# A hybrid convolution and attention block: values through DRAM, gates stored as logits, a product on GpSimd, and two PSUM banks in place of three for attention

## The chip, the cores and the metric

The kernel runs on one NeuronCore of a Trainium2 chip. The metric is the device time of one execution in microseconds (us). Five engines work side by side, each through its own queue in order: TensorE (PE, with its weight loads shown as PEld), VectorE (DVE), ScalarE (ACT), GpSimd (POOL) and SyncE (SP), which issues the DMAs. TensorE writes into PSUM, eight banks of 512 float32 columns on 128 partitions each; every other tile lies in SBUF.

## The reference, cut to what matters

One layer over 2048 rows of 1024 channels, in float32. A projection of 7680 columns feeds two branches that are merged:

```python
h = rmsnorm(x, norm_g)
glu_in, conv_gate, q, k, v, attn_gate, merge_logits = split(h @ w_in)
c = silu(layernorm(depthwise_conv_31_taps(a * sigmoid(b))))       # a, b = halves of glu_in
y_conv = (c * silu(conv_gate)) @ w_conv_out
a = sliding_window_attention(rope(q), rope(k), v, sinks)          # 16 heads of 64, 4 key/value heads
y_attn = (a * silu(attn_gate)) @ w_attn_out                       # window 128, a sink per head
g_conv, g_attn = split(sigmoid(merge_logits))
x = x + (g_conv * y_conv + g_attn * y_attn) @ w_out
out = rmsnorm(x, final_norm_g)
```

Attention takes blocks of 128 queries against the keys of their own block and of the one before. A softmax over the window has the sink of the head in its denominator.

## The kernel before

Each float32 operand of a product is split into a rounded part and a remainder (`hi` and `lo`, both float32r), and each product is three matmuls: hi by hi, hi by lo, lo by hi. The rows are taken in two sweeps `s` of 1024 (`T`), each in two halves of 512. Channels lie on partitions, rows along the free dimension.

A sweep runs through `program()`: rotary projections of k and q and the v projection, then 32 projections of gates (`ag` for attention, `cg` for the convolution, `ma` and `mc` for the merge), with the eight channel tiles of the gated unit (`gb`, `ga`) put in between, then `ya` (attention's output product), `yc` (the convolution's) and `o` (the last). A projection of 128 columns and 512 rows is 24 matmuls into one PSUM tile of the pool `mm_ps`. Gates are activated as they leave PSUM and go to DRAM (`spill`); `load_gate` brings them back during `ya`, `yc` and in `u_op`.

The order on TensorE is the order in which the program is written. A planner, `Line`, cuts into the projections: after every three matmuls `spend` looks for work that is due, which is a step of a chain (attention, layer norm, transposes) or an operation in the background (31 vector operations for each channel tile of the convolution, whose running sum `acc` lies in two PSUM banks of `cv_ps`). The order on the other engines comes from a scheduler.

Attention is 32 units per sweep, `attention(n)`, for each key/value head `g` and query block `b`; one begins every 13.8 us by the planner's count. A unit has three steps on TensorE:

1. scores: two PSUM tiles `sc` of two heads each, four matmuls into each, one tile straight after the other. ScalarE copies one half of each into SBUF (L581), VectorE copies the other half under the causal mask (L582). Maximum, exponentials and division follow in SBUF (`ss`, `st`).
2. 22 us later four transposes into the PSUM tile `tpp`, read by ScalarE and VectorE as the hi and lo parts `pt` (L607, L242). `pc` is `pt` under a mask, made on GpSimd.
3. 16 us later the product with the values into the PSUM tile `ov`: `pt` times the values of the block before, `pc` times the difference of the two blocks' values (`vt`, `vd`). It leaves PSUM in four steps that follow one another: a copy of one half on ScalarE (L625), an addition of the other on VectorE (L626), and the same for the second pair of heads. Then the gate's product (L627), a split into hi and lo, and a store to `d_a`.

By the time that step 3 of unit n-3 is due, step 1 of unit n is due too. So `ov` of one unit and the two `sc` tiles of another stand close together on TensorE, with three projection matmuls between them or none. All of `sc`, `tpp`, `ov` and the transposes of the input and the values take their PSUM tiles from the pool `tp_ps`, which has three banks, and `mm_ps` has three.

`tile_pool(bufs=n)` gives out n buffers for one tag: a tile is written when some earlier tile's readers are done with the buffer that it gets.

Of the kernel before, what the change touches and what calls it, by code (L numbers as in the profile page):

```python
# [12 lines left out]
F32 = mybir.dt.float32  # L13
F32R = mybir.dt.float32r
I32 = mybir.dt.int32
AF = mybir.ActivationFunctionType
ALU = mybir.AluOpType
AX = mybir.AxisListType

P = 128  # L20
S = 2048
D = 1024
KC = D // P
T = 1024
NSWEEP = S // T
NB = T // P
TH = 512
TAPS = 31
HALO = TAPS - 1
HD = 64  # L30
NH = 16
NKV = 4
# [21 lines left out]
def hybrid_block(ctx: ExitStack, tc: tile.TileContext, x, par_d, w_in, w_conv, sinks, w_attn, w_out,  # L54
                 fin_g, rope_t, out):
    nc = tc.nc
# [3 lines left out]
    slots = ctx.enter_context(tc.tile_pool(name="slots", bufs=1))  # L60
    stage = ctx.enter_context(tc.tile_pool(name="stage", bufs=4))
    work = ctx.enter_context(tc.tile_pool(name="work", bufs=2))
    mm_ps = ctx.enter_context(tc.tile_pool(name="mm_ps", bufs=3, space=bass.MemoryType.PSUM))
    tp_ps = ctx.enter_context(tc.tile_pool(name="tp_ps", bufs=3, space=bass.MemoryType.PSUM))
    cv_ps = ctx.enter_context(tc.tile_pool(name="cv_ps", bufs=1, space=bass.MemoryType.PSUM))
    dram = ctx.enter_context(tc.tile_pool(name="dram", bufs=1, space=bass.MemoryType.DRAM))

# [3 lines left out]
    def f(ap):  # L71
        return ap.bitcast(F32)
# [2 lines left out]
    H = [f"h{i}" for i in range(16)]  # L75
    A = [f"a{i}" for i in range(16)]
    C = [f"c{i}" for i in range(8)]
    X = [f"x{i}" for i in range(3)]
    WIDE = set(C) | {"a14", "a15", "h14", "h15"}

    def slot(tag, shape, dt, name):
        n = int(np.prod(shape[1:]))
        full = HALO + T + 2 if tag in WIDE else 1024
        t = slots.tile([P, full], dt, tag=tag, name=name)
        v = t[:, 0:n]
        if len(shape) == 3:
            v = v.rearrange("p (a b) -> p a b", b=shape[2])
        elif len(shape) == 4:
            v = v.rearrange("p (a b c) -> p a b c", b=shape[2], c=shape[3])
        return v  # L90
# [6 lines left out]
    def next_of(key, tags):  # L97
        rot.setdefault(key, cycle(range(len(tags))))
        return tags[next(rot[key])]
# [59 lines left out]
    d_k = dram.tile([2, 2, P, S], F32, name="d_k")  # L159

    d_a = dram.tile([NSWEEP * KC, P, 2, T], F32, name="d_a")
    v_halo = const.tile([P, NKV, 2, HD], F32R, name="v_halo")
    v_last = const.tile([P, 2, P], F32, name="v_last")
    dve.memset(v_last, 0.0)

# [1 line left out]
    class Line:  # L167
        t = 0.0
# [72 lines left out]
    def split_lo(out_, full, hi, eng):  # L241
        eng.tensor_tensor(out=out_, in0=full, in1=f(hi), op=ALU.subtract)  # L242
# [129 lines left out]
    def sweep(s):  # L372
# [61 lines left out]
        def gate_item(kind, col, func, e):  # L434
            def ev(half, ps):
                g = t2k(f"{kind}{s}_{e}_{half}")
                act.activation(out=g, in_=ps, func=func)
                nc.sync.dma_start(out=spill[kind][s * KC + e, :, half * TH:(half + 1) * TH], in_=g)
                if half == 1:
                    stored.add((kind, e))  # L440

            return project(w_in[col // P + e], h_rhs, f"{kind}{s}_{e}", ev)

        def load_gate(kind, e, half):
            g = t2k(f"l{kind}{s}_{e}_{half}")
            nc.sync.dma_start(out=g, in_=spill[kind][s * KC + e, :, half * TH:(half + 1) * TH])
            return g


# [42 lines left out]
            return store  # L492


        vt, vd = {}, {}

        def v_item(i):
            def chain(half, vs):
                yield 0.0, 7.0
                tp = tp_ps.tile([P, 4, P], F32, tag="tp", name=f"tpv{s}_{i}_{half}")  # L500
                for j in range(4):
                    pe.transpose(out=tp[:, j, :], in_=vs[:, j * P:(j + 1) * P], identity=ident)
                vf, d = (t2k(f"{n}{s}_{i}_{half}").rearrange("p (b c) -> p b c", c=P) for n in ("vf", "vd"))
                act.copy(vf, tp)
                dve.tensor_tensor(out=d[:, 1:4], in0=tp[:, 1:4], in1=vf[:, 0:3], op=ALU.subtract)
                dve.tensor_tensor(out=d[:, 0], in0=tp[:, 0], in1=v_last[:, i], op=ALU.subtract)
                act.copy(v_last[:, i], vf[:, 3])
                for j in range(2):
                    bp = 2 * half + j
                    if i == 0:  # L510
                        vt[bp] = slot(AT[bp], [P, 2, NKV, 2 * HD], F32R, f"vt{s}_{bp}")
                        vd[bp] = slot((X + AT[15:])[bp], [P, 2, NKV, 2 * HD], F32R, f"vd{s}_{bp}")
                    for full, to in ((tp, vt), (d, vd)):
                        part = full[:, 2 * j:2 * j + 2, :].rearrange("p b (g d) -> p b g d", d=HD)
                        hi, lo = (to[bp][:, :, 2 * i:2 * i + 2, a * HD:(a + 1) * HD] for a in range(2))
                        act.copy(hi, part)
                        split_lo(lo, part, hi, dve)
                yield 0.44, 0.0

            def ev(half, ps):  # L520
                vs = t2k(f"vs{s}_{i}_{half}")
                act.copy(vs, ps)
                line.start(chain(half, vs))

            return project(w_in[C_V // P + i], h_rhs, f"v{i}{s}", ev)

        def v_of(g, b):
            if b < 0:
                return v_halo[:, g]
            return vt[b // 2][:, b % 2, g, :]  # L530


        done, qk = {}, {}
# [20 lines left out]
        def attention(n):  # L554
# [52 lines left out]
            act.copy(pt[:, 0], tpp)  # L607
            split_lo(pt[:, 1], tpp, pt[:, 0], dve)
            if first:
                seq = [(v_of(g, b), pt)]  # L610
            else:
                pc = slot(next_of("pc", AT[9:11]), [P, 2, GQ, P], F32R, f"pc{u}")
                pool.affine_select(out=pc, in_=f(pt), pattern=[[0, 2], [0, GQ], [1, P]],  # L613
                                   compare_op=ALU.is_ge, fill=0.0, base=0, channel_multiplier=-1)
                seq = [(v_of(g, b - 1), pt), (vd[b // 2][:, b % 2, g, :], pc)]
            yield 0.44, LAT[1]

            ov = tp_ps.tile([P, GQ, P], F32, tag="tp", name=f"ov{u}")
            nm = 2 * len(seq)
            for i in range(nm):  # L620
                vv, pp = seq[i // 2]
                pe.matmul(out=ov, lhsT=vv, rhs=pp[:, i % 2], start=(i == 0), stop=(i == nm - 1))  # L622
            ovp = ov.rearrange("p (i r) q -> p i r q", r=2)
            for r, own, other in ((0, slice(0, HD), slice(HD, P)), (1, slice(HD, P), slice(0, HD))):
                act.copy(oT[own], ovp[other, :, r, :])  # L625
                dve.tensor_tensor(out=oT[own], in0=ovp[own, :, r, :], in1=oT[own], op=ALU.add)  # L626
            dve.tensor_tensor(out=oT, in0=oT, in1=ga, op=ALU.mult)  # L627
            hl = sb.rearrange("p (l c) q -> p l c q", c=2)
            act.copy(hl[:, 0].bitcast(F32R), oT)
            split_lo(hl[:, 1].bitcast(F32R), oT, hl[:, 0], dve)  # L630
            for i in range(2):
                nc.sync.dma_start(out=d_a[e2, :, i, qs].rearrange("c p q -> p c q"), in_=hl[:, i])
            done[n] = True
            if n == NKV * NB - 1 and s + 1 < NSWEEP:
                pool.tensor_copy(out=v_halo, in_=f(vt[NB // 2 - 1][:, 1]).rearrange(
                    "p g (a d) -> p g a d", d=HD))
            yield nm * MM_US, 0.0

        def start_attention():
            load_qk(0)  # L640
            for n in range(NKV * NB):
                line.after(22.0 + n * ATT_EVERY, attention(n),
                           lambda n=n: n not in begun or ("ag", 2 * (n // NB) + 1) in stored)
            line.every = CONV_EVERY
            start_tail()
# [14 lines left out]
        def ln_stats(parts, name):  # L660

            st = []
            for half in range(2):
                st.append(mm_ps.tile([P, TH], F32, tag="mm", name=f"{name}{s}_{half}"))
                for i in range(2):
                    pe.matmul(out=st[half], lhsT=ones, rhs=parts[half][i], start=(i == 0), stop=(i == 1))
            return st
# [22 lines left out]
        def ln_chain():  # L690
            parts = ln_parts(csum, "csum")
            yield 0.0, LN_LAT[0]
            st = ln_stats(parts, "lnmu")
            ln["mu"] = slot(X[0], [P, T], F32, f"mu{s}")
            for half in range(2):
                act.copy(ln["mu"][:, half * TH:(half + 1) * TH], st[half])
            line.every = LN_EVERY
            line.bg.extend([lambda c=c: ln_center(c) for c in range(KC)])
            line.bg.append(lambda: line.start(ln_chain2()))
            yield 4 * MM_US, 0.0  # L700

        def ln_chain2():
            parts = ln_parts(ln["v"], "vsum")
            yield 0.0, LN_LAT[1]
            st = ln_stats(parts, "lnvar")
            ln["r"] = slot(X[1], [P, T], F32, f"rstd{s}")
            for half in range(2):
                act.activation(out=ln["r"][:, half * TH:(half + 1) * TH], in_=st[half], func=AF.Sqrt, bias=eps)
            work_ops = [lambda i=i: ln_recip(i) for i in range(4)]
            line.bg.extend(work_ops + [lambda c=c: ln_apply(c) for c in range(KC)])  # L710
            line.late.append((line.t, u_chain(), lambda: len(uT) > 0))
            yield 4 * MM_US, 0.0
# [252 lines left out]
```

## Time and profile before

| | |
|---|---|
| median of 3 runs | 2053.2 us (2052.98 to 2053.33) |
| the profiled execution | 2053.2 us, of which the profile's span is 2051.5 us |
| granted TensorE clock | 0.999 |
| PE busy | 2031.3 us, 9256 matmuls |
| DVE / ACT / POOL busy | 1327.4 / 1027.8 / 403.4 us |

In a line for a group of instructions stand: line of the kernel, engine, operation, the tile written and the tiles read, shapes, count, then after a bar the busy time in us and the mean of one in ns, and after another the idle time of the engine just before them with what ended most of it. A line of the timeline has start and length in us, then the group; several equal instructions that follow each other share a line, and their length is from the first start to the last end.

### The profile page before, as it was taken

To read this page: it belongs to the slowest core of one execution; us is meant where nothing else is said; L and a number is where in the kernel's file an instruction comes from. 1 tells how busy PE (TensorE), PEld (TensorE's weight loads), DVE (VectorE), ACT (ScalarE), POOL (GpSimd) and SP (SyncE) were. 2 spreads that over 40 slices of the span, in tenths; PEclk is the share of its full clock that TensorE was granted. 3 is DMA by queue.
4 is the path that set the end of the run, shared out by engine and by line. 5 is a ranking of instruction groups with operands and counts; after the bars stand their busy time and mean duration, and the time that the engine had idled before them with its cause. 6 is when DMAs were issued, how large, how long until landed. Compare 5 with 4: busy or idle time off the path is not lost.

```text
span 2051.5 us, 27562 instructions
## 1 busy us (share of the span) xinstructions
PE 2031.3 (99%) x9256; PEld 1669.1 (81%) x9256; DVE 1327.4 (65%) x1965; ACT 1027.8 (50%) x2313; POOL 403.4 (20%) x336
## 2 busy tenths in 40 slices
PE   7999999999999999999999999999999999999998
PEld 6888888888888888888888888888888888888886
DVE  4968769988994355123668678689888924441323
ACT  6312477777777463123433125767677764621222
POOL 2335332333323223241001120111011100001200
PEclk9999999999999999999999999999999999999999
DMA  7445655555566757444344555555555577564422
GB/s 249 144 144 167 208 170 160 166 168 172 161 188 212 252 174 244 143 157 169 131 144 138 164 178 188 160 175 174 173 156 171 179 222 257 172 228 138 153 110 82
DMA packets 265821, 355.91 MB, mean 173 GB/s; under 512 B 28112, under 2 KB 126544, under 8 KB 265680
## 3 DMA queue, kind: packets, MB, share of 16 engines
q1 hardware_dynamic: 265680, 354.16, 53.3%
q8 instruction: 73, 1.20, 0.2%
q14 instruction: 68, 0.56, 0.1%
HBM read 234.51 MB, written 119.54 MB: 173 GB/s over the span
## 4 chain that ended last, share of the span: by engine, by line
PE 96%; DVE 2%; DMA 1%; issue 0%; SPq 0%; POOL 0%; ACT 0%; DVEq 0%; POOLq 0%
PE mm_cg L281 9%; PE o L885 9%; PE mm_ma L281 9%; PE mm_ga L281 9%; PE mm_mc L281 9%; PE mm_yc L281 9%; PE mm_ya L281 9%; PE mm_gb L281 8%; PE mm_ag L281 7%; PE mm_q_a L281 4%; PE mm_q_b L281 4%; PE sc L572 3%; PE ov L622 3%; PE mm_v L281 2%; DVE acc L396 2%; PE tpp L602 1%
## 5 line engine op out<-in xcount | busy, mean ns | idle before, releaser
L396 DVE SCALAR_TENSOR_TENSOR acc<-glu,par,acc 128x1024 f32<-128x1024 f32 x464 | 596.3, 1285 | 6.2
L885 PE MATMUL o<-wo,mT 128*128 128x512 f32 x768 | 181.3, 395 | 0.0
L885 PEld LDWEIGHTS o<-wo,mT 128*128 128x128 f32 x768 | 143.2, 188 | 32.0
L281 PE MATMUL mm_cg<-hT,whi_cg 128*128 128x512 f32 x512 | 161.1, 396 | 0.0
L281 PE MATMUL mm_ga<-hT,whi_ga 128*128 128x512 f32 x512 | 160.9, 395 | 0.2 <-ACT whi_ga L253 0.2
L281 PE MATMUL mm_ma<-hT,whi_ma 128*128 128x512 f32 x512 | 161.0, 396 | 0.0
L281 PE MATMUL mm_ag<-hT,whi_ag 128*128 128x512 f32 x512 | 160.8, 395 | 0.0
L281 PE MATMUL mm_gb<-hT,whi_gb 128*128 128x512 f32 x512 | 160.7, 395 | 0.0
L281 PE MATMUL mm_mc<-hT,whi_mc 128*128 128x512 f32 x512 | 159.7, 393 | 0.0
L281 PE MATMUL mm_yc<-uT,whi_yc 128*128 128x512 f32 x512 | 159.5, 393 | 0.0
L281 PE MATMUL mm_ya<-aT,whi_ya 128*128 128x512 f32 x512 | 158.7, 391 | 0.0
L613 POOL TENSOR_SCALAR_AFFINE_SELECT pc<-pt 128x1024 fp32r<-128x1024 f32 x60 | 65.6, 1094 | 428.7 <-DVE pt L242 428.6
L281 PEld LDWEIGHTS mm_yc<-uT,whi_yc 128*128 128x128 f32 x512 | 96.2, 188 | 21.8
L281 PEld LDWEIGHTS mm_mc<-hT,whi_mc 128*128 128x128 f32 x512 | 96.1, 188 | 21.7
L281 PEld LDWEIGHTS mm_ya<-aT,whi_ya 128*128 128x128 f32 x512 | 96.1, 188 | 20.9
L281 PEld LDWEIGHTS mm_ga<-hT,whi_ga 128*128 128x128 f32 x512 | 94.6, 188 | 20.4 <-ACT whi_ga L253 0.6
L281 PEld LDWEIGHTS mm_gb<-hT,whi_gb 128*128 128x128 f32 x512 | 94.7, 188 | 19.9
L281 PEld LDWEIGHTS mm_ag<-hT,whi_ag 128*128 128x128 f32 x512 | 94.3, 188 | 19.4
L281 PEld LDWEIGHTS mm_cg<-hT,whi_cg 128*128 128x128 f32 x512 | 94.2, 188 | 19.5
L281 PEld LDWEIGHTS mm_ma<-hT,whi_ma 128*128 128x128 f32 x512 | 94.2, 188 | 19.3
L592 ACT ACTIVATE ss<-ss,st 128x128 f32<-128x128 f32 x256 | 99.7, 391 | 11.2 <-DVE st L587 10.7
L281 PE MATMUL mm_ga<-hT,wlo_ga 128*128 128x512 f32 x256 | 100.8, 394 | 0.7 <-POOL wlo_ga L242 0.7
(364 smaller groups left out, 4259.3 us busy)
## 6 DMA issues: line engine op xcount, KB each, us to landing
qk<-d_q SPq DMA_DIRECT2D x256, 64.0 KB, 2.2
d_a<-ss SPq DMA_DIRECT2D x128, 128.0 KB, 1.9
aT<-d_a SPq DMA_DIRECT2D x32, 512.0 KB, 5.5
qk<-d_k SPq DMA_DIRECT2D x240, 64.0 KB, 2.0
raw_gb<-in_w_in_dram SPq DMA_DIRECT2D x34, 256.0 KB, 3.2
raw_ga<-in_w_in_dram SPq DMA_DIRECT2D x34, 256.0 KB, 3.3
raw_ag<-in_w_in_dram SPq DMA_DIRECT2D x32, 256.0 KB, 3.7
d_ag<-ag SPq DMA_DIRECT2D x32, 256.0 KB, 2.2
```

The source lines that it names most:

```text
L281: pe.matmul(out=ps, lhsT=a, rhs=b, start=(k == 0 and i == 0), stop=(k == KC - 1 and i == 2))
L396: dve.scalar_tensor_tensor(out=to, in0=glu[c][:, j:j + T], scalar=tap(c, j), in1=acc[c], op0=ALU.mult, op1=ALU.add)
L572: pe.matmul(out=o, lhsT=q[:, h, :], rhs=r, start=(j == 0), stop=(j == 1))
L592: act.activation(out=sb[:, h, :], in_=sb[:, h, :], func=AF.Exp, scale=SCALE, bias=ngm[:, h:h + 1], accum_out=den[:, h:h + 1])
L602: pe.transpose(out=tpp[:, h, :], in_=sb[:, h, :], identity=ident)
L613: pool.affine_select(out=pc, in_=f(pt), pattern=[[0, 2], [0, GQ], [1, P]], compare_op=ALU.is_ge, fill=0.0, base=0, channel_multiplier=-1)
L622: pe.matmul(out=ov, lhsT=vv, rhs=pp[:, i % 2], start=(i == 0), stop=(i == nm - 1))
L885: pe.matmul(out=ps, lhsT=a[:, c0:c0 + P], rhs=r, start=(k == 0 and i == 0), stop=(k == KC - 1 and i == 2))
```

## The change

- Values: the hi and lo parts of the values and of their differences are no longer kept in SBUF for the sweep. Each half of each v projection is stored to DRAM (`d_v`), and `load_v` brings back the values of four blocks of one head at a time into one buffer, `vg`. The load for the next four is issued after the `ov` matmuls of every fourth unit. `v_halo`, which carried the last block over to the next sweep, goes.
- Gates: `cg`, `ma` and `mc` are copied out of PSUM as logits and stored so; `load_gate` activates them after the load, on ScalarE. `ag` stays as it was.
- Attention's gate product and the remainder of its split move from VectorE to GpSimd.
- PSUM: `mm_ps` has four banks, `tp_ps` has two. The layer norm's sums (`lnmu`, `lnvar`) move from `mm_ps` to `tp_ps`.
- Slots: the tags `x0` to `x2` go; the mean lies in `a14` and the reciprocal deviation in the buffer `ln0` of `csum`.

```diff
-    mm_ps = ctx.enter_context(tc.tile_pool(name="mm_ps", bufs=3, space=bass.MemoryType.PSUM))
-    tp_ps = ctx.enter_context(tc.tile_pool(name="tp_ps", bufs=3, space=bass.MemoryType.PSUM))
+    mm_ps = ctx.enter_context(tc.tile_pool(name="mm_ps", bufs=4, space=bass.MemoryType.PSUM))
+    tp_ps = ctx.enter_context(tc.tile_pool(name="tp_ps", bufs=2, space=bass.MemoryType.PSUM))
...
         def gate_item(kind, col, func, e):
...
-                act.activation(out=g, in_=ps, func=func)
+                act.activation(out=g, in_=ps, func=func if kind == "ag" else AF.Copy)
...
         def load_gate(kind, e, half):
...
+            act.activation(out=g, in_=g, func=AF.Silu if kind == "cg" else AF.Sigmoid)
...
         def v_item(i):
...
-                        hi, lo = (to[bp][:, :, 2 * i:2 * i + 2, a * HD:(a + 1) * HD] for a in range(2))
-                        act.copy(hi, part)
-                        split_lo(lo, part, hi, dve)
+                b0 = s * NB + 4 * half
+                for n, full in enumerate((tp, d)):
+                    to = slot(next_of("hl", AT[7:11]), [P, 4, 2, 2 * HD], F32R, f"v{'td'[n]}{s}_{i}_{half}")
+                    part = full.rearrange("p b (g d) -> p b g d", d=HD)
+                    act.copy(to[:, :, :, 0:HD], part)
+                    split_lo(to[:, :, :, HD:], part, to[:, :, :, 0:HD], dve)
+                    nc.sync.dma_start(out=d_v[n, i, b0:b0 + 4].rearrange("b p g d -> p b g d"), in_=f(to))
...
+        def load_v(n):
+            if n >= NKV * NB:
+                return
+            g, b = divmod(n, NB)
+            blk = s * NB + b
+            t = vg[n // 4] = slot(AT[15], [P, 2, 4, 2 * HD], F32R, f"vg{s}_{n}")
+            j0 = 1 if blk == 0 else 0
+            nc.sync.dma_start(out=f(t[:, 0, j0:]),
+                              in_=d_v[0, g // 2, blk - 1 + j0:blk + 3, :, g % 2].rearrange("b p d -> p b d"))
+            nc.sync.dma_start(out=f(t[:, 1]),
+                              in_=d_v[1, g // 2, blk:blk + 4, :, g % 2].rearrange("b p d -> p b d"))
...
-                vv, pp = seq[i // 2]
-                pe.matmul(out=ov, lhsT=vv, rhs=pp[:, i % 2], start=(i == 0), stop=(i == nm - 1))
+                w, j, pp = seq[i // 2]
+                pe.matmul(out=ov, lhsT=vg[n // 4][:, w, j], rhs=pp[:, i % 2], start=(i == 0), stop=(i == nm - 1))
+            if n % 4 == 3:
+                load_v(n + 1)
...
-            dve.tensor_tensor(out=oT, in0=oT, in1=ga, op=ALU.mult)
+            pool.tensor_tensor(out=oT, in0=oT, in1=ga, op=ALU.mult)
...
-            split_lo(hl[:, 1].bitcast(F32R), oT, hl[:, 0], dve)
+            split_lo(hl[:, 1].bitcast(F32R), oT, hl[:, 0], pool)
...
-                st.append(mm_ps.tile([P, TH], F32, tag="mm", name=f"{name}{s}_{half}"))
+                st.append(tp_ps.tile([P, TH], F32, tag="tp", name=f"{name}{s}_{half}"))
```

On TensorE the change moves nothing: matmul for matmul the order is the one of before, and only the operands of `ov` have other names. Here is the place where unit g=2, b=2 of the first sweep has its third step (`ov_2_2`) and unit b=5 its first (`sc_2_5_0`, `sc_2_5_1`). Behind a row stand the semaphores that it waits for, by the engine that raises them. Before:

```order
L622 MATMUL ov_2_2_4828<-pc_2_2_4670,vd_1_766 128x512 [waits Pool_49]
L622 MATMUL ov_2_2_4828<-pc_2_2_4670,vd_1_766 128x512
L281 MATMUL mm_cg_60_4793<-hT_0_7_131,whi_cg_61_4649 128x512 x2
L281 MATMUL mm_cg_60_4793<-hT_0_7_131,wlo_cg_61_4650 128x512
L572 MATMUL sc_2_5_0_4857<-qk_21_4703 128x256 [waits DMAHW4_49,DMAHW5_49,DMAHW3_49,DMAHW6_49,DMAHW2_49,DMAHW7_49,DMAHW0_49,DVE_49]
L572 MATMUL sc_2_5_0_4857<-qk_21_4703 128x256 x3
L572 MATMUL sc_2_5_1_4862<-qk_21_4703 128x256 [waits DVE_49]
L572 MATMUL sc_2_5_1_4862<-qk_21_4703 128x256 x3
```

The same place of TensorE's order after the change:

```order
L626 MATMUL ov_2_2_4835<-pc_2_2_4677,vg_16_4416 128x512 [waits Pool_49]
L626 MATMUL ov_2_2_4835<-pc_2_2_4677,vg_16_4416 128x512
L280 MATMUL mm_cg_60_4800<-hT_0_7_131,whi_cg_61_4656 128x512 x2
L280 MATMUL mm_cg_60_4800<-hT_0_7_131,wlo_cg_61_4657 128x512
L576 MATMUL sc_2_5_0_4864<-qk_21_4710 128x256 [waits DMAHW3_49,DMAHW4_49,DMAHW2_49,DMAHW5_49,DMAHW1_49,DMAHW6_49,DMAHW0_49,DVE_49]
L576 MATMUL sc_2_5_0_4864<-qk_21_4710 128x256 x3
L576 MATMUL sc_2_5_1_4869<-qk_21_4710 128x256 [waits DVE_49,PE_49]
L576 MATMUL sc_2_5_1_4869<-qk_21_4710 128x256 x3
```

What moved is the target of the second score tile's wait for VectorE: before it is the split of `pt` that frees `tpp`, here it is the second addition that frees `ov_2_2`, four matmuls of which stand just ahead. VectorE's order shows where that addition stands (`acc` is the convolution, `ss<-causal,sc` the masked copies of the scores). Before, both masked copies come ahead of the second addition:

```order
L242 TENSOR_TENSOR pt_2_3_4809<-tpp_2_3_4803,pt_2_3_4809 128x512
L396 SCALAR_TENSOR_TENSOR acc_6_5087<-glu_6_4473,par,acc_6_5087 128x1024 x2
L626 TENSOR_TENSOR ss_2_2_4440<-ov_2_2_4828,ss_2_2_4440 64x256
L582 COPY_PREDICATED ss_2_5_4867<-causal,sc_2_5_0_4857 128x256
L582 COPY_PREDICATED ss_2_5_4867<-causal,sc_2_5_1_4862 128x256
L626 TENSOR_TENSOR ss_2_2_4440<-ov_2_2_4828,ss_2_2_4440 64x256
```

VectorE at the same place after the change:

```order
L241 TENSOR_TENSOR pt_2_3_4816<-tpp_2_3_4810,pt_2_3_4816 128x512
L395 SCALAR_TENSOR_TENSOR acc_6_5097<-glu_6_4480,par,acc_6_5097 128x1024 x2
L632 TENSOR_TENSOR ss_2_2_4447<-ov_2_2_4835,ss_2_2_4447 64x256
L395 SCALAR_TENSOR_TENSOR acc_6_5097<-glu_6_4480,par,acc_6_5097 128x1024
L632 TENSOR_TENSOR ss_2_2_4447<-ov_2_2_4835,ss_2_2_4447 64x256
L586 COPY_PREDICATED ss_2_5_4874<-causal,sc_2_5_0_4864 128x256
L395 SCALAR_TENSOR_TENSOR acc_6_5097<-glu_6_4480,par,acc_6_5097 128x1024
L586 COPY_PREDICATED ss_2_5_4874<-causal,sc_2_5_1_4869 128x256
```

The second addition now stands ahead of both masked copies, with one operation of the convolution between it and the first addition. In other units the scheduler gives the second score tile the bank of the first instead, so that it waits for that tile's masked copy: in 32 of the 64 units it waits so, in 26 for the second addition of `ov`, and in the 6 others, which stand at the beginning of a sweep, nothing stands close ahead of it or it waits for nothing recent.

More of the change, by code (lines that the diff above doesn't have):

```diff
@@ L77, in hybrid_block @@
     C = [f"c{i}" for i in range(8)]
-    X = [f"x{i}" for i in range(3)]
-    WIDE = set(C) | {"a14", "a15", "h14", "h15"}
+    WIDE = set(C) | {"a14"}
     def slot(tag, shape, dt, name):
@@ L161, in hybrid_block @@
     d_a = dram.tile([NSWEEP * KC, P, 2, T], F32, name="d_a")
-    v_halo = const.tile([P, NKV, 2, HD], F32R, name="v_halo")
+    d_v = dram.tile([2, 2, S // P, P, 2, 2 * HD], F32, name="d_v")
     v_last = const.tile([P, 2, P], F32, name="v_last")
@@ L492, in store_q @@
             return store
-        vt, vd = {}, {}
         def v_item(i):
@@ L507, in chain @@
                 act.copy(v_last[:, i], vf[:, 3])
[L508 to L514, printed above, removed]
-                        hi, lo = (to[bp][:, :, 2 * i:2 * i + 2, a * HD:(a + 1) * HD] for a in range(2))
-                        act.copy(hi, part)
-                        split_lo(lo, part, hi, dve)
+                b0 = s * NB + 4 * half
[5 more added lines that the diff above has]
+                    nc.sync.dma_start(out=d_v[n, i, b0:b0 + 4].rearrange("b p g d -> p b g d"), in_=f(to))
                 yield 0.44, 0.0
@@ L525, in v_item @@
             return project(w_in[C_V // P + i], h_rhs, f"v{i}{s}", ev)
[L527 to L530, printed above, removed]
+        vg = {}
+        def load_v(n):
[9 more added lines that the diff above has]
+                              in_=d_v[1, g // 2, blk:blk + 4, :, g % 2].rearrange("b p d -> p b d"))
         done, qk = {}, {}
@@ L609, in attention @@
             if first:
-                seq = [(v_of(g, b), pt)]
+                seq = [(0, 1, pt)]
             else:
@@ L614, in attention @@
                                    compare_op=ALU.is_ge, fill=0.0, base=0, channel_multiplier=-1)
-                seq = [(v_of(g, b - 1), pt), (vd[b // 2][:, b % 2, g, :], pc)]
+                seq = [(0, b % 4, pt), (1, b % 4, pc)]
             yield 0.44, LAT[1]
@@ L633, in attention @@
             done[n] = True
-            if n == NKV * NB - 1 and s + 1 < NSWEEP:
-                pool.tensor_copy(out=v_halo, in_=f(vt[NB // 2 - 1][:, 1]).rearrange(
-                    "p g (a d) -> p g a d", d=HD))
             yield nm * MM_US, 0.0
@@ L640, in start_attention @@
             load_qk(0)
+            load_v(0)
             for n in range(NKV * NB):
@@ L693, in ln_chain @@
             st = ln_stats(parts, "lnmu")
-            ln["mu"] = slot(X[0], [P, T], F32, f"mu{s}")
+            ln["mu"] = slot(AT[14], [P, T], F32, f"mu{s}")
             for half in range(2):
@@ L705, in ln_chain2 @@
             st = ln_stats(parts, "lnvar")
-            ln["r"] = slot(X[1], [P, T], F32, f"rstd{s}")
+            ln["r"] = work.tile([P, T], F32, tag="ln0", name=f"rstd{s}", bufs=1)
             for half in range(2):
```

## The prediction

> **What bounds the kernel now.** I read the page's busy times and its chain first, then TensorE's list of waits, then the timeline of single attention units.
>
> ```profile
> PE 2031.3 (99%) x9256; PEld 1669.1 (81%) x9256; DVE 1327.4 (65%) x1965; ACT 1027.8 (50%) x2313; POOL 403.4 (20%) x336
> ...
> PE 96%; DVE 2%; DMA 1%; issue 0%; SPq 0%; POOL 0%; ACT 0%; DVEq 0%; POOLq 0%
> ```
>
> TensorE is busy for 2031.3 of 2051.5 us, and the chain that ended last is TensorE for 96% of it. Matmuls overlap in this count, so it doesn't say that TensorE is at its peak. It does say that nothing else holds it up. The list of TensorE's waits, whole:
>
> ```profile
> PE tpf L361 <- DVE ident_r L117: 8.4, 1, 8.4
> PE tpf L361 <- DVE xf L354: 2.4, 2, 1.5
> PE sc L572 <- DVE pt L242: 1.0, 1, 1.0
> PE mm_ga L281 <- POOL wlo_ga L242: 0.7, 1, 0.7
> PE tpf L361 <- DVE hT L364: 0.5, 1, 0.5
> PE mm_ga L281 <- ACT whi_ga L253: 0.2, 1, 0.2
> ```
>
> That is 13.2 us, all but one in the first 27 us. None is a projection that waits for a bank of its pool. The 1.0 is a score tile that waits for the bank of `tpp`. So there is little to win, and each wait that is put into TensorE's order later on is paid in full, for no idle time follows that could take it up.
>
> **The change part by part.** TensorE's instructions and their order stay, so only waits can change the time. The part that adds them is the third bank taken from attention. With two banks the second score tile needs the bank of its own first tile or that of the `ov` just ahead. This is such a place, from `ov_2_1` to the scores of the unit three further on:
>
> ```profile
> 503.88 0.62 PE L622 MATMUL ov<-pt,vt 128*128 128x512 f32 x2
> 504.34 0.64 PE L622 MATMUL ov<-pc,vd 128*128 128x512 f32 x2
> 504.82 0.63 PE L281 MATMUL mm_cg<-hT,whi_cg 128*128 128x512 f32 x2
> 505.02 0.37 ACT L625 COPY ss<-ov 64x256 f32<-64x256 f32 x1 [3.12 <-PE ov L622]
> ...
> 505.52 1.11 PE L572 MATMUL sc<-qk 128*128 128x256 f32 x8
> 505.91 0.41 DVE L626 TENSOR_TENSOR ss<-ov,ss 64x256 f32<-64x256 f32 x1
> ...
> 506.46 0.63 PE L281 MATMUL mm_cg<-hT,whi_cg 128*128 128x512 f32 x2
> ...
> 508.25 0.43 DVE L626 TENSOR_TENSOR ss<-ov,ss 64x256 f32<-64x256 f32 x1
> ```
>
> Eight score matmuls take 506.46 - 505.52 = 0.94 us, so the second tile starts at 505.99. `ov` is read out at 508.25 + 0.43 = 508.68. Before, that was no matter; now a tile which gets this bank would stand 2.7 us, were nothing reordered. A unit that is less disturbed, with no projection between, shows the links by themselves:
>
> ```profile
> 1657.17 0.64 PE L622 MATMUL ov<-pc,vd 128*128 128x512 f32 x2
> 1657.65 1.12 PE L572 MATMUL sc<-qk 128*128 128x256 f32 x8
> 1657.85 0.37 ACT L625 COPY ss<-ov 64x256 f32<-64x256 f32 x1 [1.22 <-PE ov L622]
> 1658.25 0.42 DVE L626 TENSOR_TENSOR ss<-ov,ss 64x256 f32<-64x256 f32 x1 [3.10 <-ACT ss L625]
> 1658.33 0.37 ACT L581 COPY ss<-sc 128x256 f32<-128x256 f32 x1
> 1658.60 0.63 PE L281 MATMUL mm_ma<-hT,whi_ma 128*128 128x512 f32 x2
> 1658.73 0.45 DVE L582 COPY_PREDICATED ss<-causal,sc 128x256 f32<-128x256 int32 x1
> ```
>
> Hand-overs cost little: copy to addition 0.03 us here, and 0.05 from VectorE's end to TensorE at the one wait of this kind, 351.24 + 0.68 to 351.97:
>
> ```profile
> 351.24 0.68 DVE L242 TENSOR_TENSOR pt<-tpp,pt 128x512 fp32r<-128x512 f32 x1
> ...
> 351.97 0.74 PE L572 MATMUL sc<-qk 128*128 128x256 f32 x4 [0.97 <-DVE pt L242]
> 352.55 0.63 PE L281 MATMUL mm_gb<-hT,whi_gb 128*128 128x512 f32 x2
> ```
>
> *Class a*, 32 units, in which the second tile waits for the masked copy of the first. That copy ends at 1658.73 + 0.45 = 1659.18; TensorE goes on at 1659.23 instead of 1657.65 + 0.48 = 1658.13. That is 1.10 us, and it doesn't depend on projections between, since both ends follow the first tile. 32 x 1.10 = 35.
>
> *Class b*, 26 units, in which it waits for `ov`'s second addition. From the copy at 505.02, with the lengths above: first addition done at 505.84. Where the scheduler leaves a convolution operation between the two additions, its mean counts:
>
> ```profile
> L396 DVE SCALAR_TENSOR_TENSOR acc<-glu,par,acc 128x1024 f32<-128x1024 f32 x464 | 596.3, 1285 | 6.2
> L626 DVE TENSOR_TENSOR ss<-ov,ss 64x256 f32<-64x256 f32 x128 | 53.7, 420 | 70.2 <-ACT ss L625 68.3
> ```
>
> 505.84 + 1.28 + 0.42 + 0.05 = 507.59, 1.60 after 505.99. 13 units are so: 21. In 5 more no projection stands between, the tile is due 0.70 earlier (505.52 - 504.82), and the wait is 2.30: 11.5. In 8 units the additions follow each other. There ScalarE's second copy (0.37) and the addition end at 506.74, a wait of 0.75, or, if ScalarE copies the first score tile in between (due 0.68 after the tile's start, as in the second unit), at 507.47, a wait of 1.48. I take 1.2: 9.6. Together 42.
>
> *Lateness.* VectorE wasn't ready at 505.42, when the first copy was done, but at 505.91: two convolution operations stood ahead. The line above has VectorE idle for 70.2 us before 128 additions, so it is often there in time and often not. GpSimd takes two operations of each unit over, and the new waits give VectorE further time. I take 0.3 us for 58 units: 17, between 0 and the 0.49 of the unit shown, 28.
>
> *Other users of the two banks.* The transposes at the start (16 tiles) run against a readout of 0.69 and 0.75 us:
>
> ```profile
> L364 DVE SCALAR_TENSOR_TENSOR hT<-tpf,par,hT 128x512 fp32r<-128x512 f32 x16 | 11.8, 750 | 12.7 <-ACT hT L363 12.5
> L363 ACT ACTIVATE hT<-tpf,par 128x512 fp32r<-128x512 f32 x16 | 10.8, 686 | 4.7 <-PE tpf L361 4.5
> ```
>
> With four transposes of 0.1 to 0.2 us, two tiles take 2.0 to 2.4 us through two banks, one per 1.0 to 1.2 instead of per 0.75. That is at most 8 x 0.45 = 3.6 for the first eight, of which the waits of 0.7 and 0.2 for weights would take up 0.9. I take 1, as later tiles stand between matmuls. The layer norm's four pairs of sums now follow `ov` or each other in these banks: 0 to 4 x 1.1, I take 2. The first score tile now waits for `tpp`, 0.48 us earlier than the second did: 0 to 3, I take 1.
>
> *What I cost at nothing.* The fourth projection bank: no such wait is in the list. The gate's product and split on GpSimd: its operation of 1024 columns takes 2.41 us, so 0.6 each for 256, beside 0.51 on VectorE; behind them in its queue stand weight splits for a projection that is one ahead of TensorE's, and in SP's queue the store to `d_a`, which is read only after the last unit.
>
> ```profile
> L402 POOL TENSOR_TENSOR csum<-csum,cv 128x1024 f32<-128x1024 f32 x14 | 33.7, 2410 | 63.9 <-DVE cv L396 26.3 <-DVE st L594 21.9 <-DVE st L587 8.2
> L627 DVE TENSOR_TENSOR ss<-ss 128x256 f32<-128x256 f32 x64 | 32.6, 509 | 0.2
> L437 ACT ACT_TABLE_LOAD x60 | 77.0, 1283 | 1.1
> L437 ACT ACTIVATE cg<-mm_cg 128x512 f32<-128x512 f32 x32 | 19.1, 597 | 5.8 <-PE mm_cg L281 5.5
> lma<-d_ma SPq DMA_DIRECT2D x32, 256.0 KB, 4.0
> 764.00:940.00 176.00, 176.00 (x768) 143.99 (x767) 62.37 (x85) 47.93 (x75) 60.25 (x45) 1.00 0.54 182
> ```
>
> Logits: 154 table loads become 94, so 60 x 1.283 = 77 us leave ScalarE, mostly in attention, where no wait of TensorE hangs on it. 96 activations of 0.60 = 57 us come in `ya` and `yc`, where ScalarE is busy for 47.9 of 176 us (the window above). Each stands behind a DMA of 4.0 us, and the weight casts behind it are a projection ahead. If that cover failed, each would hold TensorE by a part of 4 us, and there are four projection banks to bridge it. The values: as many elements are split as before, 8 stores are added and 64 loads issued on SP's queue; between the first store and the first load stand all projections of q.
>
> The sum is 35 + 42 + 17 + 4 = 98 us. The profiled execution took 2053.2, the same as the median, so 2053.2 + 98 = 2151.
>
> **Rivals.** *The clock falls.* A transpose at the start shows a slow TensorE, although the granted clock reads 1.00 there:
>
> ```profile
> 12.19 1.27 PE L361 MATMUL tpf<-ident_r,xf 128*128 128x128 f32 x5
> 28.18 0.60 PE L361 MATMUL tpf<-ident_r,xf 128*128 128x128 f32 x4
> ```
>
> Five take 1.27 us at first and four 0.60 at 28 us. The last one's own run of some 0.3 is in both, so they start about 0.24 apart and then 0.10. If each of 58 waits brought that back for the 6.5 us that it lasted then (from 12.2 until projections run at their pace at 18.7), 58 x 3.2 = 186 us would come on top: 2337. Against it, the wait of 0.97 at 351.97 left no slow matmuls behind it: the four score matmuls there took 352.55 - 351.97 = 0.58 us, against 0.47 for four in the units above, 0.1 more and not twice as much. [...] I give it 4%.
>
> *The values come late.* `vg` is one buffer, and its two DMAs are issued after the fourth `ov`. One product is due 14.1 us after another:
>
> ```profile
> 518.02 0.62 PE L622 MATMUL ov<-pt,vt 128*128 128x512 f32 x2
> SPq L632 <- ACT ss L629: 62.9, 54, 4.1
> ```
>
> A DMA of this size lands in about 4 us, two in 5. SP's queue waits 4.1 at its longest for the store of a unit, which now comes later. 14.1 - 1.1 for the product itself - 5 - 4.1 leaves 4 us; only above that does TensorE wait. 14 reloads late by 5 us more would add 70: 2221. 5%.
>
> *No slower.* The second score tile gets a bank that is free already, because `ov` has been read out by then; this decides at a readout within 1.0 us of the end of `ov` (504.98 to 505.99). The fastest links give 0.04 + 0.37 + 0.03 + 0.42 + 0.03 + 0.37 + 0.03 + 0.42 = 1.7, and only 26 units wait for that; the other 32 would still give 35 us. Only if the first tile were freed within its own four matmuls would the time be 2053. 3%.
>
> *Less than summed.* Additions without convolution between, no lateness: 35 + 26 x 0.75 = 55, so 2108. 8%. The sum as forecast has 80%.
>
> **Range.** Low: 55 plus a little of the 4, 2110. High: 35 + 26 x 2.7 (the readout as it ran at 508.68) + 28 + 4 = 137, so 2190. The two rivals above it stay out, with 9%. Slower by over 0.2% has 0.96, and within 0.2% and faster share the rest at 0.03 and 0.01. 0.2% is 4 us, about what a measurement of this kernel tells from no change.
>
> **What would show it.** The waits of TensorE: `sc` behind the masked copy of `sc` (some 32, 1.1 us and up) and behind the addition of `ov` (some 26, 0.8 to 2.7), 80 to 120 us in all, and no line for a projection's bank. Matmuls keep their spacing, and stretches without attention their length. I am wrong if `ov` waits for the load of `vg`, if projections wait for weights whose casts or splits stand behind a gate or a product, or if matmuls after a wait lie further apart.

## The result and the profile after

| | before | after |
|---|---|---|
| median | 2053.2 us (2052.98 to 2053.33) | 2161.9 us (2160.38 to 2163.02) |
| the profiled execution | 2053.2 us, span 2051.5 | 2163.0 us, span 2161.3 |
| granted TensorE clock | 0.999 | 0.993 |

The change makes the kernel slower: 1.0529 times the time before, with an interval of 1.0511 to 1.0547. The forecast was 2151, in a range of 2110 to 2190.

The first lines of the page of after answer to those of before: busy time by engine, and the chain that ended last, by engine.

```profile
PE 2062.9 (95%) x9256; PEld 1681.2 (78%) x9256; DVE 1290.2 (60%) x1821; ACT 999.9 (46%) x2333; POOL 496.0 (23%) x463
...
PE 85%; DVE 9%; ACT 3%; issue 3%; DMA 1%; POOL 0%; DVEq 0%; SPq 0%; ACTq 0%; POOLq 0%
```

TensorE runs the same 9256 matmuls, but it is busy for 95% of the span instead of 99%. The chain now leaves it for VectorE (9%) and ScalarE (3%): some other engine's work stands between two of its matmuls. Its own busy time has grown too, by 31.6 us. Part of that is arithmetic (a score matmul runs for 0.28 us and the next starts 0.12 us after it, but one that waited no longer overlaps the one before), and part is a clock that fell for a while, to a mean of 0.993, shown below.

TensorE's waits of after, whole; the numbers are us in total, times, and the longest:

```profile
PE sc L576 <- DVE ss L632: 39.1, 26, 2.2
PE sc L576 <- DVE ss L586: 36.2, 32, 2.2
PE tpf L360 <- DVE ident_r L116: 8.4, 1, 8.4
PE tpf L360 <- DVE hT L363: 2.4, 4, 0.7
PE mm_ya L280 <- ACT whi_ya L252: 2.1, 1, 2.1
PE tpf L360 <- DVE xf L353: 1.7, 2, 0.9
PE lnmu L670 <- ACT mu L700: 0.7, 1, 0.7
PE mm_ya L280 <- POOL wlo_ya L241: 0.6, 1, 0.6
PE sc L576 <- DVE pt L241: 0.2, 1, 0.2
```

The first two lines are the classes b and a of the prediction, 26 and 32 times, 75.3 us together. No projection waits for a bank, and `ov` never waits for the load of its values. The two lines of `mm_ya` are new and were not forecast.

TensorE's order is the same in both kernels, so the distance from the start of one matmul to the start of the next can be compared pair by pair. That splits the 109.8 us by which the span grew:

| where | us |
|---|---|
| second score tile, class a (32) | 40.2 |
| second score tile, class b (26) | 43.3 |
| one matmul further: the first after each wait takes longer | 5.2 |
| eight stretches at half the clock, seven in attention and one in `ya` | 12.4 |
| `mm_ya` outside those | 6.2 |
| transposes at the start | 2.2 |
| layer norm 0.9, first score tiles 0.7 | 1.6 |
| all else | −1.3 |

The two classes are larger here than in the list of waits (83.5 against 75.3), because the list counts from the end of the last matmul, whose run of 0.28 us outlasts the 0.12 us to the next one, and the prediction counted from start to start.

A class a unit of after, in the timeline (start, length, engine, line, operation; in brackets the idle time ahead and what ended it):

```profile
503.64 0.74 PE L576 MATMUL sc<-qk 128*128 128x256 f32 x4
...
503.69 0.37 ACT L631 COPY ss<-ov 64x256 f32<-64x256 f32 x1 [1.42 <-PE ov L626]
...
504.45 0.37 ACT L585 COPY ss<-sc 128x256 f32<-128x256 f32 x1 [0.40 <-PE sc L576]
504.69 0.41 DVE L632 TENSOR_TENSOR ss<-ov,ss 64x256 f32<-64x256 f32 x1
...
505.02 0.43 DVE L586 COPY_PREDICATED ss<-causal,sc 128x256 f32<-128x256 int32 x1
505.13 0.36 ACT L631 COPY ss<-ov 64x256 f32<-64x256 f32 x1 [0.30 <-DVE ss L632]
505.51 0.74 PE L576 MATMUL sc<-qk 128*128 128x256 f32 x4 [1.14 <-DVE ss L586]
```

The first score tile starts at 503.64, ScalarE copies its half from 504.45, VectorE the other from 505.02 to 505.45, and TensorE goes on at 505.51. In the unit of before that the prediction quotes, the second tile began 0.48 us after the first; here it begins 1.87 us after it. VectorE's first addition to `ov` stands between and costs this unit the 0.2 us from 504.82, when ScalarE's copy is done, to 505.02.

A class b unit, with what came behind it:

```profile
1558.73 0.63 PE L576 MATMUL sc<-qk 128*128 128x256 f32 x4
1558.93 0.37 ACT L631 COPY ss<-ov 64x256 f32<-64x256 f32 x1 [1.44 <-PE ov L626]
1559.34 0.42 DVE L632 TENSOR_TENSOR ss<-ov,ss 64x256 f32<-64x256 f32 x1 [0.86 <-ACT ss L631]
1559.68 1.27 DVE L395 SCALAR_TENSOR_TENSOR acc<-glu,par,acc 128x1024 f32<-128x1024 f32 x1
...
1560.98 0.43 DVE L632 TENSOR_TENSOR ss<-ov,ss 64x256 f32<-64x256 f32 x1
...
1561.55 0.71 PE L576 MATMUL sc<-qk 128*128 128x256 f32 x4 [2.19 <-DVE ss L632]
...
1563.85 1.05 PE L280 MATMUL mm_cg<-hT,whi_cg 128*128 128x512 f32 x2
...
1566.91 0.40 PE L280 MATMUL mm_cg<-hT,wlo_cg 128*128 128x512 f32 x1
1567.14 0.62 PE L280 MATMUL mm_cg<-hT,whi_cg 128*128 128x512 f32 x2
```

The second addition to `ov` ends at 1561.41 since one convolution operation of 1.27 us stands ahead of it, and TensorE stands for 2.19 us. Then two things follow. The four score matmuls take 0.71 instead of 0.63 us. And from 1563.0 the projection's matmuls start 0.43 us apart (two of them: 1.05 instead of 0.62) until 1566.4, after which they are back at 0.23. In the answer by stretches, the number behind the counts of the five engines is the granted clock:

```profile
1563.00:1566.40 3.40, 3.40 (x9) 2.60 (x8) 3.40 (x6) 0.00 (x0) 0.49 (x1) 0.51 0.64 146
1566.50:1570.00 3.50, 3.50 (x17) 2.84 (x16) 2.53 (x3) 1.97 (x9) 0.00 (x0) 1.00 0.42 142
```

Nine matmuls run in the first stretch and 17 in the second: the clock was halved for one stretch of 3.4 us. While TensorE works, after has eight of these (from 552.7, 631.2, 853.1, 1433.3, 1481.1, 1528.9, 1563.0 and 1580.1 us; the one at 853.1 is in `ya`); their starts lie whole multiples of 3.413 us apart, and each costs some 1.5 us.

### The profile page after: what moved, and what is told of

It reads as the page before. It is cut to its first block, busy times and chain, and to the rows that moved or that the text cites. A ratio compares the mean times of both kernels' runs of the same rounds, so it can differ in the third digit from the quotient of the medians.

```text
span 2161.3 us, 27912 instructions
## 1 busy us (share of the span) xinstructions
PE 2062.9 (95%) x9256; PEld 1681.2 (78%) x9256; DVE 1290.2 (60%) x1821; ACT 999.9 (46%) x2333; POOL 496.0 (23%) x463
## 4 chain that ended last, share of the span: by engine, by line
PE 85%; DVE 9%; ACT 3%; issue 3%; DMA 1%; POOL 0%; DVEq 0%; SPq 0%; ACTq 0%; POOLq 0%
PE o L889 8%; PE mm_yc L280 8%; PE mm_ga L280 8%; PE mm_mc L280 8%; PE mm_gb L280 8%; PE mm_ma L280 8%; PE mm_cg L280 7%; PE mm_ya L280 7%; DVE acc L395 5%; PE mm_ag L280 4%; PE mm_q_a L280 4%; PE mm_q_b L280 4%; PE sc L576 3%; PE ov L626 2%; PE mm_v L280 2%
## 5 line engine op out<-in xcount | busy, mean ns | idle before, releaser
L576 PE MATMUL sc<-qk 128*128 128x256 f32 (+1 forms) x512 | 86.3, 293 | 75.7 <-DVE ss L632 39.1
L576 PEld LDWEIGHTS sc<-qk 128*128 128x128 f32 x512 | 73.3, 190 | 92.9 <-DVE ss L586 42.6
L241 DVE TENSOR_TENSOR pt<-tpp,pt 128x512 fp32r<-128x512 f32 x64 | 43.9, 686 | 121.7 <-ACT pt L611 121.6
L632 DVE TENSOR_TENSOR ss<-ov,ss 64x256 f32<-64x256 f32 x128 | 53.9, 421 | 99.9 <-ACT ss L631 98.0
```

Of the source, the lines that this page charges most:

```text
L576: pe.matmul(out=o, lhsT=q[:, h, :], rhs=r, start=(j == 0), stop=(j == 1))
```

## The experiments

Theory 1 is that of the prediction: nearly all of the cost is the second score tile that waits for one of two banks. Against it stood that the other parts of the change share the cost (values that come late, the logits' activations on ScalarE, the product on GpSimd), and that what a wait costs is more than its length, because the clock falls behind it.

**The banks: given back, and taken alone.** The first kernel is after with three banks for each pool, the second is before with four and two.

```diff
-    mm_ps = ctx.enter_context(tc.tile_pool(name="mm_ps", bufs=4, space=bass.MemoryType.PSUM))
-    tp_ps = ctx.enter_context(tc.tile_pool(name="tp_ps", bufs=2, space=bass.MemoryType.PSUM))
+    mm_ps = ctx.enter_context(tc.tile_pool(name="mm_ps", bufs=3, space=bass.MemoryType.PSUM))
+    tp_ps = ctx.enter_context(tc.tile_pool(name="tp_ps", bufs=3, space=bass.MemoryType.PSUM))
```

> The changed kernel with three banks for each pool again; values, logits and GpSimd's product stay as changed. Bank theory: the waits of score tiles (75 us), the 0.1 us that TensorE loses at each of them and the half-clock stretches that follow some of them go; what is left is the wait of mm_ya for its weights (2.7 us) with the half-clock stretch behind it (1.5 us), so 2053 to 2059 us. Rival theory (the moved work makes the readouts late, and the banks only show it): other waits come up in their place, 2075 us or more.

> The kernel before with four banks for projections and two for attention, nothing else. Bank theory: 58 waits of score tiles of 1 us and up, some more than after the change, as VectorE still has the gate product and ScalarE its table loads: 75 to 100 us of waits, 6 us of slow restarts, 10 to 25 us of half clock: 2145 to 2180 us. Rival theory: the waits come from the moved work, so below 2110 us.

With three banks the changed kernel takes 2060.6 us (2058.95 to 2062.43), 1.0038 of before (1.0025 to 1.0052). That is a little above what theory 1 allowed. With two banks and nothing else changed, before takes 2142.4 us (2141.05 to 2143.64), 1.0434 (1.0418 to 1.0451), a little below it. TensorE's largest waits, other than the start's 8.4 us, in the kernel with three banks:

```profile
PE mm_ya L280 <- DVE mp L803: 5.4, 3, 3.1
PE tpf L360 <- DVE xf L353: 2.1, 2, 1.2
```

and in before with two:

```profile
PE sc L572 <- DVE ss L582: 37.6, 34, 2.3
PE sc L572 <- DVE ss L626: 33.5, 24, 2.4
```

The third bank alone makes 89 of the 109 us, and giving it back takes away all waits of `sc`. Both misses point the same way: some 7 us or more of the change are not the banks, and in the first kernel they lie in `ya`, where two stretches at half the clock follow a wait of 3.1 us (the granted clock is 0.998 over the whole span).

**One bank.** After with five banks for projections and one for attention.

```diff
-    mm_ps = ctx.enter_context(tc.tile_pool(name="mm_ps", bufs=4, space=bass.MemoryType.PSUM))
-    tp_ps = ctx.enter_context(tc.tile_pool(name="tp_ps", bufs=2, space=bass.MemoryType.PSUM))
+    mm_ps = ctx.enter_context(tc.tile_pool(name="mm_ps", bufs=5, space=bass.MemoryType.PSUM))
+    tp_ps = ctx.enter_context(tc.tile_pool(name="tp_ps", bufs=1, space=bass.MemoryType.PSUM))
```

> The changed kernel with one bank for attention and five for projections, to see waits of twice the size. Each unit waits twice: the first score tile for ov's readout (1.7 to 2.7 us after ov, less the projections between), the second for the first tile's masked copy (1.1 us and up). 64 x 1.1 + 58 x 1.7 = 170 us of waits, 12 of restarts, 8 at the start. If TensorE's clock is halved for 3.4 us after a 3.4 us stretch with over 1.9 us idle, both waits lie in one stretch in most units, so 40 to 60 stretches of 1.5 us follow: 2300 to 2360 us. If the half clock came by chance as often as after the change (8 stretches), 2240 to 2290 us.

It takes 2428.2 us (2425.45 to 2429.5), 1.1822 (1.1804 to 1.184), with a granted clock of 0.941: more than either theory gave. From its list of waits, and the granted clock of the page's 40 slices in tenths:

```profile
PE sc L576 <- issue: 116.4, 58, 3.7
PE sc L576 <- DVE ss L586: 84.3, 64, 2.6
PE tpf L360 <- DVE hT L363: 14.2, 14, 2.1
...
PEclk9999988888988999999999999899998988999999
```

Now both score tiles of nearly every unit wait (58 and 64 times). The list names nothing that ends the 58 waits of the first tile; each of them ends 0.10 us after VectorE's second addition to an `ov`. Compared pair by pair with before, 222 of the 376 us by which the span is longer are these score waits, 109 lie in stretches at half the clock, 16 are the transposes at the start and 9 the first matmuls behind a wait. A granted clock of 0.941 over the span of 2427.8 us comes to some 286 us at half, if all else ran at 1.00. So the clock is lower where the waits are more: 0.941 with 200.7 us of waits for score tiles, 0.993 with after's 75.3.

**The distance between `ov` and the scores.** After with step 3 of a unit due 13 us behind step 2 instead of 16, so that `ov` stands some 3 us further ahead of the scores. There are still two banks.

```diff
-LAT = (22.0, 16.0)
+LAT = (22.0, 13.0)
```

> The changed kernel, two banks, with the planner's wait ahead of the product with the values 13 us instead of 16. That puts 12 or 18 projection matmuls (2.8 to 4.1 us) between ov and the next score tiles in place of 0 or 3. Bank theory: ov has been read out by then (1.7 to 3.7 us after its end), the second score tile finds a free bank, and the time is 2053 to 2065 us with two banks. If the readouts were late as such (rival theory), the wait would only move, 2100 us or more.

It takes 2076.1 us (2075.85 to 2076.38), 1.0113 (1.0099 to 1.0128): 86 us of the 109 are gone with the banks left as they are. The time lies 11 us above the range that was expected: ten waits for `ov` stayed, and `ya` still waits:

```profile
PE sc L576 <- DVE ss L632: 7.6, 10, 1.3
...
PE mm_ya L280 <- ACT whi_ya L252: 2.0, 1, 2.0
PE mm_ya L280 <- POOL wlo_ya L241: 1.2, 2, 0.6
PE sc L576 <- DVE ss L586: 1.1, 1, 1.1
```

Class a all but vanishes as well, 1 time instead of 32. With `ov` out of the way both banks are free when the scores begin, and the second tile doesn't have to take the bank of the first. So two banks are not too few in themselves; they are too few for three tiles that follow each other within some 2 us. Until TensorE has finished, no stretch at half the clock is left in this trace, whose granted clock is 1.0 and whose longest wait in attention is 1.3 us. The whole list of waits is 13.6 us longer than before's, of the 22.5 us by which the span is; TensorE's order differs here, so the rest can't be told pair by pair.

**A fourth bank for attention.** Before with two banks for projections and four for attention.

```diff
-    mm_ps = ctx.enter_context(tc.tile_pool(name="mm_ps", bufs=3, space=bass.MemoryType.PSUM))
-    tp_ps = ctx.enter_context(tc.tile_pool(name="tp_ps", bufs=3, space=bass.MemoryType.PSUM))
+    mm_ps = ctx.enter_context(tc.tile_pool(name="mm_ps", bufs=2, space=bass.MemoryType.PSUM))
+    tp_ps = ctx.enter_context(tc.tile_pool(name="tp_ps", bufs=4, space=bass.MemoryType.PSUM))
```

> The kernel before with two banks for projections and four for attention. A projection fills a bank for 5.5 us and its readout takes under 2 us, so bank theory sees no wait of a projection; the one wait of a score tile (1.0 us) and the 0.5 us of the transposes at the start go: 2051 to 2053.2 us. Rival: projections wait for readouts that stand behind a convolution operation on VectorE, 2055 us or more.

It takes 2073.9 us (2070.58 to 2075.71), 1.0101 (1.0086 to 1.0115). I had expected no change, and that was wrong:

```profile
PE mm_mc L281 <- ACT mc L437: 5.6, 3, 2.5
PE mm_ga L281 <- ACT whi_ga L253: 4.4, 1, 4.4
...
PE lnvar L666 <- ACT rstd L708: 2.1, 2, 1.2
PE mm_ya L281 <- DVE mp L799: 1.8, 1, 1.8
```

A projection with two banks waits until ScalarE has activated the tile two before it (`mc`). Some 6 us more lie in four stretches at half the clock, behind waits of `mm_ga`, `mm_mc` and `mm_ya`; the granted clock is 0.995. So in this kernel three banks for projections are needed, three for attention are needed, and that a fourth isn't waited for says nothing on whether a third can be spared.

**The logits alone.** Before with the gates stored as logits.

```diff
-                act.activation(out=g, in_=ps, func=func)
+                act.activation(out=g, in_=ps, func=func if kind == "ag" else AF.Copy)
...
+            act.activation(out=g, in_=g, func=AF.Silu if kind == "cg" else AF.Sigmoid)
```

> The kernel before with cg, ma and mc stored as logits and activated after the load, nothing else. Theory: the wait of mm_ya for a readout that stands behind the activation and a table load, some 5 us, and a half-clock stretch of 2.4 us behind it, as with three banks after the change: 2058 to 2063 us, and no wait in attention. Rival: the cost needs the other parts too, 2053 to 2055 us.

It takes 2061.4 us (2061.0 to 2062.33), 1.0041 (1.0028 to 1.0054), 8 us more. The prediction had this at nothing.

```profile
PE mm_ya L281 <- DVE mp L800: 4.0, 4, 1.7
...
PE mm_ya L281 <- POOL wlo_ya L242: 1.3, 2, 0.6
```

With three projection banks `ya` waits for `mp`, the product of a gate with a projection's result, which frees the projection's bank; the gate is now late. With four banks (after) that wait is gone, and a weight cast behind the activations is late instead. From the timeline of after:

```profile
845.92 1.28 ACT L446 ACT_TABLE_LOAD   x1 [1.50 <-DMA lma<-d_ma]
...
848.89 1.28 ACT L446 ACT_TABLE_LOAD   x1
850.19 0.63 ACT L446 ACTIVATE lcg<-lcg 128x512 f32<-128x512 f32 x1
850.72 0.60 ACT L252 CAST whi_ya<-raw_ya 128x512 fp32r<-128x512 f32 x1
851.38 0.73 PE L280 MATMUL mm_ya<-aT,whi_ya 128*128 128x512 f32 x2 [2.12 <-ACT whi_ya L252]
851.40 1.28 POOL L241 TENSOR_TENSOR wlo_ya<-raw_ya,whi_ya 128x512 fp32r<-128x512 f32 x1 [11.38 <-ACT whi_ya L252]
852.74 0.52 PE L280 MATMUL mm_ya<-aT,wlo_ya 128*128 128x512 f32 x1 [0.63 <-POOL wlo_ya L241]
```

The cast of `whi_ya` stands in ScalarE's queue behind the loads and activations of two gates, and GpSimd's split behind the cast: TensorE waits 2.12 and then 0.63 us. From 844.42, when ScalarE had last finished an operation, to the cast at 850.72 it stood 1.50 us at a gate's DMA, spent 2.57 us on two table loads and the rest on activations and casts. What ScalarE itself waits for in after, from 780 to 960 us:

```profile
ACT lmc L446 <- DMA lmc<-d_mc: 37.2, 11, 5.4
...
ACT lma L446 <- DMA lma<-d_ma: 9.5, 4, 4.9
```

An activation that stands behind its gate's DMA holds all of ScalarE's queue for up to 5.4 us. The long ones come from 864 us on, and TensorE doesn't stop for them; the wait of `ya` needed only the 1.50 us and the table loads. ScalarE has the time for the work (it is busy for 91.0 of the 176 us from 765 to 941); the cost lies in what stands ahead of the cast.

**The values and the product on GpSimd alone.** After with three banks each and the gates activated as before.

```diff
-    mm_ps = ctx.enter_context(tc.tile_pool(name="mm_ps", bufs=4, space=bass.MemoryType.PSUM))
-    tp_ps = ctx.enter_context(tc.tile_pool(name="tp_ps", bufs=2, space=bass.MemoryType.PSUM))
+    mm_ps = ctx.enter_context(tc.tile_pool(name="mm_ps", bufs=3, space=bass.MemoryType.PSUM))
+    tp_ps = ctx.enter_context(tc.tile_pool(name="tp_ps", bufs=3, space=bass.MemoryType.PSUM))
...
-                act.activation(out=g, in_=ps, func=func if kind == "ag" else AF.Copy)
+                act.activation(out=g, in_=ps, func=func)
...
-            act.activation(out=g, in_=g, func=AF.Silu if kind == "cg" else AF.Sigmoid)
```

> The changed kernel with three banks for each pool and with all gates activated as they leave PSUM, as before; values through DRAM and the product on GpSimd stay. If the 7.5 us that three banks left (2060.6) come from the activations after the load, the waits of mm_ya for readouts and weights go, and the time is 2052.5 to 2054.5 us. If values or the product have a share, 2056 to 2060 us.

It takes 2054.9 us (2054.44 to 2055.62), 1.0009 (1.0 to 1.0017). This lies between the two expectations and within 0.2% of before: some 2 us are left for the values, the product, the layer norm's moved sums and the slots together, between 0 and 3.5 by the interval. No matmul waits for the values or the product in its trace.

**The product on VectorE.** After with the product and the split back on VectorE.

```diff
-            pool.tensor_tensor(out=oT, in0=oT, in1=ga, op=ALU.mult)
+            dve.tensor_tensor(out=oT, in0=oT, in1=ga, op=ALU.mult)
...
-            split_lo(hl[:, 1].bitcast(F32R), oT, hl[:, 0], pool)
+            split_lo(hl[:, 1].bitcast(F32R), oT, hl[:, 0], dve)
```

> The changed kernel with attention's gate product and split back on VectorE, two banks for attention. By the prediction GpSimd frees VectorE and so shortens the readouts: waits of score tiles of 80 to 95 us and 2167 to 2180 us with VectorE. By the run with two banks alone, where 71 us of waits stood with the product on VectorE, it does nothing for them: 2150 to 2164 us.

It takes 2158.0 us (2156.74 to 2160.79), 1.0512 (1.0498 to 1.0527), no more than after.

```profile
PE sc L576 <- DVE ss L632: 42.1, 29, 2.3
PE sc L576 <- DVE ss L586: 29.9, 29, 1.9
```

72.0 us of waits with VectorE doing the work, 75.3 with GpSimd doing it. That GpSimd's help shortens the readouts, as the prediction said, is not borne out.

The parts add up: banks 89.3 (before with two), logits 8.1, values and product 1.7, together 99 of the 108.7 us. Compared pair by pair, after is 20.1 us longer than before with two banks: 8.7 lie in stretches at half the clock (eight of them instead of two, a granted clock of 0.993 instead of 0.997), 6.2 in `ya` and 4.6 in score waits that are longer. So the other 10 us are there only when the parts come together; no run separates why more stretches at half the clock come then.

## Why the prediction was right, and which terms were off

*The mechanism and its links: right.* The waits are where they were forecast and as often, 26 and 32 times, and the runs with the banks back and with `ov` moved away show that they are the cost.

| term | forecast | measured |
|---|---|---|
| class a, bare | 32 x 1.10 = 35 | most units 1.14 |
| class b, bare | 13 x 1.60, 5 x 2.30, 8 x 1.2 = 42 | of the 13: nine at 1.64 to 1.73, three late ones at 2.17 to 2.30, one at 1.29; the 5 at 2.35; of the 8: seven at 0.84 to 1.11, one late one at 2.12 |
| lateness | 17 | 83.5 − 77 = 6.5 |
| other users of the banks | 4 | 2.2 + 0.9 + 0.7 = 3.8 |
| slower matmuls behind a wait | 0 | 5.2 + 12.4 = 17.6 |
| `ya` (`mm_ya`) | 0 | 6.2 |

The three kinds of class b stand 13, 5 and 8 times, as forecast. Where nothing is late, the waits come out within 0.05 us for class a and the 5, and within 0.13 for nine of the 13; the 8 are mostly below the 1.2 that was taken.

*Lateness: too high by 10.* VectorE is more often in time than the unit at 503.88 of before let expect. In after it is idle ahead of the additions to `ov` for longer than before's 70.2 us:

```profile
L632 DVE TENSOR_TENSOR ss<-ov,ss 64x256 f32<-64x256 f32 x128 | 53.9, 421 | 99.9 <-ACT ss L631 98.0
```

The waits themselves give it most of that time: in before with two banks alone it is 92.6 us, and in after with three banks 78.1. In 42 of the 58 units VectorE adds within 0.1 us of ScalarE's copy. The estimate took a unit that ran late for the usual case, though the row of idle times spoke against it.

*The matmul's pace behind a wait: taken as unchanged, costs 17.6.* The wait at 351.97 of before was read rightly as no fall of the clock, but it was 0.97 us long, and it was carried over to waits of up to 2.2 us. The 0.1 us by which the four matmuls behind it ran longer was in the row and was left out of the sum; 58 of these make the 5.2 us. The clock rival thus came true in part: 12 us of its 186, since the clock halves for one stretch of 3.413 us, behind 7 of the 58 waits and once in `ya`. Its price was read from the start of before, where the view gives a clock of 1.00; but the trace has no record of the clock there until 17.68 us, and such time counts as full clock. The transposes start 0.21 us apart until 17.3 us and 0.11 from 18.4 on, so their slow pace looks like half the clock. In the trace of after, the 3.413 us ahead of each halved stretch held 1.92 to 2.34 us of TensorE's idle time. If that trace is divided into pieces of 3.413 us, counted from the halved ones, from the clock's first record at 23.64 us until TensorE has finished, every piece that no halved one followed held 1.50 us at most. Three waits of over 2.1 us in attention lay across two such pieces, with up to 1.50 in each, and no halved one followed. What sets the clock, no run shows.

*The logits: at nothing, 8 by themselves.* "The weight casts behind it are a projection ahead" failed: in a queue that runs in order, a stand of 1.50 us at a DMA and two table loads of 1.28 us, with the activations behind them, used up that lead once in `ya`. Of the 6.2 us, 3.1 are the two waits, from start to start; the other 3.1 are spread over all matmuls of `ya`, which start 232.6 ns apart on the mean instead of 228.7. That is no cost of the logits: the distance is 228.8 with the logits alone and 228.7 with two banks alone, but 232.6 with values and product and 232.5 with the product back on VectorE. So it belongs to the values, the layer norm's sums or the slots; which of them, and why, stays open.

*Costed at nothing, and nearly so it was:* the values through DRAM and the product on GpSimd, some 2 us together with the moved sums and the slots. The fourth projection bank only swaps one wait in `ya` for another.

So the total came out 11 us above the forecast by errors of both signs: 10 too much for lateness and 24 too little for the pace and for `ya`; the remaining 2.5 are other tiles and the profiled execution, which lies 1.2 above the median. That the total is this close is partly luck; the two classes of waits are not. Of the three signs that the prediction named for being wrong, `ov` waiting for its values didn't show, and the other two did: weights behind a gate, and matmuls further apart behind a wait.

## What to carry to other kernels

Count PSUM banks by the tiles that follow each other closely on TensorE, not by how many are in use on the mean: where three tiles came within some 2 us and each took 1 to 2 us to be read out, two banks cost a wait nearly every time, and moving one of the tiles some 3 us away gave back 86 us where the third bank gave back 101. Operations that follow a DMA in an engine's queue hold up what stands behind them (ScalarE's stood for up to 5.4 us here), so work moved to its place of use has to be judged by the queue's order there and not by the engine's idle share. And add to a wait of TensorE what comes behind it: in after 5.2 us for the restarts at 58 waits, some 0.09 us each, and 12.4 us for eight stretches at half the clock, some 1.5 us each.

## What the runs showed of the hardware that was not expected

- In after the granted clock goes to half eight times before TensorE has finished, for 3.413 us each, in which 128x512 matmuls start 0.43 us apart instead of 0.23. TensorE had been idle for 1.92 to 2.34 of the 3.413 us ahead. In before, whose one wait in attention was 0.97 us long, the clock stays at 1.00 from its first record until TensorE has finished.
- With one bank for attention, and 200.7 us of waits for score tiles instead of 75.3, the granted clock is 0.941 instead of 0.993.
- In after the first score matmul behind a wait takes mostly 0.07 to 0.10 us more than its like, and four of them take 0.71 to 0.74 us instead of 0.63.
- One part of the waits that TensorE's list leaves out: 0.15 us each, by which a matmul's run outlasts the distance to the next one. 83.5 us from start to start stand against 75.3 in the list.
